# RMSNorm with SiLU: another division of the work over the engines, and loads and stores on two queues

## The chip, the cores and the metric

The kernel runs on one core of a Trainium2 chip. The time is the device time in microseconds of one execution; lower is better. The engines' names in the profile are PE (TensorE), DVE (VectorE), ACT (ScalarE), POOL (GpSimd) and SP (SyncE). They run side by side, each works through its own instructions in their order, and they wait for each other by semaphores. Transfers between HBM and the on-chip memory are done by 16 DMA engines; SP and ACT only issue them.

## The reference

The input x has 8 x 1024 rows of 2048 float32 values. Each row is divided by its root mean square, multiplied by gamma, and passed through SiLU:

```python
rms = np.sqrt(np.mean(x ** 2, axis=-1, keepdims=True) + eps)
out = gamma * x / rms
return (out * (1 / (1 + np.exp(-out)))).astype(np.float32)
```

67.1 MB are read and 67.1 MB written.

## The kernel before

The 8192 rows are cut into 16 blocks (`nblk`) of 512 rows. A block is one tile `xt` of 128 partitions with J = 4 rows each, 4.19 MB, so every partition holds 32 KB that lie together in HBM. The tile is loaded, changed in place and stored. There are 6 such buffers (`BUFS`), and `LEAD` = 5 blocks are loaded ahead.

The work on a block has two parts. `stats(b)` makes the reciprocal root mean square: ACT squares rows 0 to 2 and sums them (L63), DVE does row 3 with a fused multiply and reduce (L59); both write their squares to PSUM tiles that nobody reads. POOL then turns the four sums into the variance (L66) and raises it to the power -0.5 (L69). `finish(b)` multiplies each row by rstd and gamma in one instruction on DVE (L74), and after each second row ACT applies Silu to a pair of rows at once, 4096 values per partition (L78). Then SP issues the store (L79).

The order is written out by hand, under `manual_schedule`: each engine runs its instructions in the order of the program text. The main loop calls `stats(b + 1)` before `finish(b)`, so ACT and DVE sum up the squares of the next block before they finish this one, and rstd of a block is made one step ahead of its use. After `finish(b)` comes `load(b + 5)`.

All loads and stores of x are issued by SP on one queue, in program order. `load(b + 5)` waits until the buffer that it takes is free, which is when store b - 1 has landed; the store of the next block stands behind that wait. Gamma is loaded by ACT's queue into one row of the first buffer and spread over the 128 partitions by POOL (L89).

Of the kernel before, what the change touches and what calls it, by code (L numbers as in the profile page):

```python
# [1 line left out]

# [4 lines left out]

ACT = mybir.ActivationFunctionType
ALU = mybir.AluOpType


@with_exitstack
def kernel(
    ctx: ExitStack,
    tc: tile.TileContext,
    x: bass.AP,
    gamma: bass.AP,
    eps: bass.AP,
    out: bass.AP,
):  # L20

    nc = tc.nc
    P = nc.NUM_PARTITIONS
    f32 = mybir.dt.float32
    x2 = x.flatten_outer_dims()
    o2 = out.flatten_outer_dims()
    n, d = x2.shape
    J = 4  # L30
    BUFS, LEAD = 6, 5
    nblk = n // (P * J)
    xb = x2.rearrange("(b p j) d -> b p (j d)", p=P, j=J)
    ob = o2.rearrange("(b p j) d -> b p (j d)", p=P, j=J)

    singles = ctx.enter_context(tc.tile_pool(name="singles", bufs=1))
    pool = ctx.enter_context(tc.tile_pool(name="pool", bufs=BUFS))
    small = ctx.enter_context(tc.tile_pool(name="small", bufs=4))
    psum = ctx.enter_context(tc.tile_pool(name="psum", bufs=1, space=bass.MemoryType.PSUM))

    g = singles.tile([P, d], f32)
    half = singles.tile([P, J], f32)
    junk_a = psum.tile([P, d], f32, name="junk_a")
    junk_v = psum.tile([P, d], f32, name="junk_v")
    blocks, rstds = {}, {}

    def load(b):
        xt = pool.tile([P, J * d], f32, name="xt")
        nc.sync.dma_start(out=xt, in_=xb[b])  # L49
        blocks[b] = xt  # L50

    def row(b, j):
        return blocks[b][:, j * d:(j + 1) * d]

    def stats(b):
        ss = small.tile([P, J], f32, name="ss")
        for j in range(J):
            if j == J - 1:
                nc.vector.tensor_tensor_reduce(  # L59
                    out=junk_v, in0=row(b, j), in1=row(b, j), scale=1.0, scalar=0.0,  # L60
                    op0=ALU.mult, op1=ALU.add, accum_out=ss[:, j:j + 1])
            else:
                nc.scalar.activation(out=junk_a, in_=row(b, j), func=ACT.Square,  # L63
                                     accum_out=ss[:, j:j + 1])
        var = small.tile([P, J], f32, name="var")
        nc.gpsimd.tensor_scalar(out=var, in0=ss, scalar1=1.0 / d, scalar2=float(eps),  # L66
                                op0=ALU.mult, op1=ALU.add)
        rstd = small.tile([P, J], f32, name="rstd")
        nc.gpsimd.tensor_tensor(out=rstd, in0=var, in1=half, op=ALU.pow)  # L69
        rstds[b] = rstd  # L70

    def finish(b):
        for j in range(J):
            nc.vector.scalar_tensor_tensor(out=row(b, j), in0=row(b, j), scalar=rstds[b][:, j:j + 1],  # L74
                                           in1=g, op0=ALU.mult, op1=ALU.mult)
            if j % 2:
                pair = blocks[b][:, (j - 1) * d:(j + 1) * d]
                nc.scalar.activation(out=pair, in_=pair, func=ACT.Silu)  # L78
        nc.sync.dma_start(out=ob[b], in_=blocks.pop(b))  # L79
        del rstds[b]  # L80

    with tc.manual_schedule():
        grow = pool.tile([P, J * d], f32, name="xt")
        nc.scalar.dma_start(out=grow[0:1, 0:d],
                            in_=bass.AP(tensor=gamma.tensor, offset=gamma.offset, ap=[[d, 1], gamma.ap[0]]))
        for b in range(LEAD):
            load(b)
        nc.gpsimd.memset(half, -0.5)  # L88
        nc.gpsimd.partition_broadcast(g, grow[0:1, 0:d])  # L89
        stats(0)  # L90
        for b in range(nblk):
            if b + 1 < nblk:
                stats(b + 1)
            finish(b)
            if b + LEAD < nblk:
                load(b + LEAD)


# [1 line left out]
_INS = ['x', 'gamma', 'eps']  # L100
_OUTS = [((8, 1024, 2048), 'float32')]

_NUMBERS = {'eps': 9.999999747378752e-06}


# [26 lines left out]
```

## Time and profile before

| | us |
|---|---|
| median of 8 runs | 320.78 (320.63 to 321.87) |
| the profiled execution, its own time | 320.71 |
| span of the profiled execution | 318.9 |
| busy: DVE, ACT, POOL | 181.9, 213.1, 60.2 |
| a 4.19 MB transfer, issue to landing, median: load, store | 29.4, 38.4 |
| first load lands, first store is issued, last store is issued | 13.6, 40.2, 293.5 |

The span is the time from the first to the last thing that the profile records; the reported time is 1.8 us longer. A row of the profile's groups gives line, engine, operation, output and inputs with their shapes, how many there were, their busy time and mean duration in ns, and then how long the engine stood idle before them and what ended most of that. The chain of waits follows the work that ended last backwards: at each step to what released it. A queue's line gives its packets, megabytes and its share of the time of the 16 DMA engines.

### The profile page before, as it was taken

The numbers are of one execution on the slowest core, as the hardware profiler recorded it, in microseconds if no ns is written. First come the engines' busy times: TensorE is split into PE (matmuls) and PEld (weight loads), VectorE is DVE, ScalarE is ACT, GpSimd is POOL, SyncE is SP. The second block draws the span as 40 slices with busy tenths as digits, with TensorE's granted clock in tenths as the row PEclk, the third lists the DMA queues.
The fourth block names the chain that finished last, engine by engine and source line by source line (L and its number), as shares of the span: only waits on it lengthen the run. The fifth ranks groups of instructions, "written<-read, shape, count | busy, mean of one in ns | idle before, by whom it ended". The sixth has DMA issues, their size and how long they took to land.

```text
span 318.9 us, 433 instructions
## 1 busy us (share of the span) xinstructions
DVE 181.9 (57%) x96; ACT 213.1 (67%) x130; POOL 60.2 (19%) x38
## 2 busy tenths in 40 slices
DVE  0208998898629185391854909458093672993000
ACT  1249899999988478384784748757487674876000
POOL 0206324502104004040030402204021040400000
DMA  8999999999999999999999999999999999999993
GB/s 322 423 423 452 403 460 353 436 444 419 448 419 424 452 411 452 407 449 432 423 452 411 440 427 436 440 419 444 423 432 444 415 452 419 440 440 415 456 415 164
DMA packets 4612, 134.24 MB, mean 421 GB/s; under 512 B 513, under 2 KB 513, under 8 KB 513
## 3 DMA queue, kind: packets, MB, share of 16 engines
q1 hardware_dynamic: 4608, 134.22, 98.3%
q14 instruction: 2, 0.02, 0.0%
q10 hardware_dynamic: 2, 0.01, 0.0%
HBM read 67.12 MB, written 67.11 MB: 421 GB/s over the span
## 4 chain that ended last, share of the span: by engine, by line
DMA 74%; DVE 8%; ACT 5%; issue 3%; DVEq 1%; SPq 1%; POOL 0%; ACTq 0%; POOLq 0%
DMA out_dram<-xt 58%; DMA xt<-in_x_dram 16%; DVE xt L74 8%; ACT xt L78 3%; ACT junk_a L63 3%; DVEq L127 1%; SPq L49 1%; POOL rstd L69 0%; DVE ss L59 0%; DVE junk_v L59 0%; DVEq L74 0%; ACTq L63 0%; DVEq L59 0%; SPq L79 0%; POOLq L66 0%
## 5 line engine op out<-in xcount | busy, mean ns | idle before, releaser
L74 DVE SCALAR_TENSOR_TENSOR xt<-xt,rstd,g 128x2048 f32<-128x2048 f32 x64 | 146.1, 2346 | 3.4 <-POOL rstd L69 3.4
L78 ACT ACTIVATE xt<-xt 128x4096 f32<-128x4096 f32 x32 | 115.2, 3613 | 20.8 <-DVE xt L74 20.8
L63 ACT ACTIVATE junk_a<-xt 128x2048 f32<-128x2048 f32 x48 | 90.2, 1880 | 58.2 <-DMA xt<-in_x_dram 57.2
L59 DVE CUSTOM_DVE_ANT_0 junk_v<-xt 128x2048 f32<-128x2048 f32 x16 | 36.8, 2299 | 104.6 <-DMA xt<-in_x_dram 104.6
L66 POOL TENSOR_SCALAR var<-ss 128x4 f32<-128x4 f32 x16 | 19.6, 1226 | 207.1 <-ACT junk_a L63 185.0
L69 POOL TENSOR_TENSOR rstd<-var,half 128x4 f32<-128x4 f32 x16 | 38.0, 2376 | 1.3
L63 ACT ACTIVATION_READ_ACCUMULATOR junk_a<-xt 128x1 f32 x48 | 8.9, 186 | 0.0
L89 POOL PARTITION_BROADCAST g<-xt x1 | 2.3, 2302 | 10.2 <-issue 10.2
L59 DVE DVE_READ_ACCUMULATOR2_ANT ss<- 128x1 f32 x16 | 2.3, 141 | 0.0
L63 ACT ACT_TABLE_LOAD x1 | 1.3, 1283 | 1.3 <-PEq L113 1.3
L78 ACT ACT_TABLE_LOAD x1 | 1.3, 1283 | 0.0
L88 POOL MEMSET half<- 128x4 f32 x1 | 0.1, 102 | 0.3 <-POOLq L113 0.3
L113 POOL MEMSET const-float32-0.0<- 128x1 f32 x1 | 0.1, 99 | 0.2 <-issue 0.2
L113 POOL MEMSET const-bfloat16-1.0<- 128x1 bf16 x1 | 0.1, 103 | 0.0
L113 POOL MEMSET const-uint8-127<- 128x1 uint8 x1 | 0.1, 102 | 0.0
L113 POOL MEMSET const-float32-1.0<- 128x1 f32 x1 | 0.1, 99 | 0.0
## 6 DMA issues: line engine op xcount, KB each, us to landing
xt<-in_x_dram SPq DMA_DIRECT2D x16, 4096.0 KB, 29.4
out_dram<-xt SPq DMA_DIRECT2D x16, 4096.0 KB, 38.4
xt<-in_gamma_dram ACTq DMA_DIRECT2D x1, 8.0 KB
```

Source lines behind the costliest of these rows:

```text
L49: nc.sync.dma_start(out=xt, in_=xb[b])
L59: nc.vector.tensor_tensor_reduce(out=junk_v, in0=row(b, j), in1=row(b, j), scale=1.0, scalar=0.0, op0=ALU.mult, op1=ALU.add, accum_out=ss[ ...
L63: nc.scalar.activation(out=junk_a, in_=row(b, j), func=ACT.Square, accum_out=ss[:, j:j + 1])
L66: nc.gpsimd.tensor_scalar(out=var, in0=ss, scalar1=1.0 / d, scalar2=float(eps), op0=ALU.mult, op1=ALU.add)
L69: nc.gpsimd.tensor_tensor(out=rstd, in0=var, in1=half, op=ALU.pow)
L74: nc.vector.scalar_tensor_tensor(out=row(b, j), in0=row(b, j), scalar=rstds[b][:, j:j + 1], in1=g, op0=ALU.mult, op1=ALU.mult)
L78: nc.scalar.activation(out=pair, in_=pair, func=ACT.Silu)
L88: nc.gpsimd.memset(half, -0.5)
L89: nc.gpsimd.partition_broadcast(g, grow[0:1, 0:d])
L113: nc = _bacc.Bacc("TRN2", target_bir_lowering=False, num_devices=1)
L127: with _tile.TileContext(nc) as tc:
```

## The change

- The third square of a block moves from ACT to DVE: ACT sums rows 0 and 1, DVE rows 2 and 3.
- rstd is made on DVE: variance, a first guess from the bits of the number (a shift and a subtraction), and four Newton steps of three instructions each, 15 instructions on 128 x 4 values.
- DVE multiplies a row by gamma alone; rstd is the scale operand of Silu on ACT, so that Silu runs row by row, four per block instead of two.
- There is no look-ahead any more: one function `work(b)` does squares, rstd, multiplications, Silu and store of one block, and the loop calls it block after block.
- Stores are issued by ACT, after a block's last Silu. SP issues only loads. `LEAD` is 6: load b + 6 takes the buffer of block b and waits for its store. The sixth load is issued at the start behind gamma's use, since gamma's row lies in that buffer.
- Gamma is spread over the partitions by TensorE: four matmuls of a row of ones with 512 values of gamma into PSUM, then copied by DVE. POOL does nothing after the start.

```diff
-    BUFS, LEAD = 6, 5
+    BUFS, LEAD = 6, 6
...
-    def stats(b):
+    def rsqrt(ss):
+        var = small.tile([P, J], f32, name="var")
+        nc.vector.tensor_scalar(out=var, in0=ss, scalar1=1.0 / d, scalar2=float(eps),
+                                op0=ALU.mult, op1=ALU.add)
+        y = small.tile([P, J], f32, name="y")
+        t = small.tile([P, J], f32, name="t")
+        nc.vector.tensor_single_scalar(out=t.bitcast(i32), in_=var.bitcast(i32), scalar=1,
+                                       op=ALU.logical_shift_right)
+        nc.vector.tensor_scalar(out=y.bitcast(i32), in0=t.bitcast(i32), scalar1=-1, scalar2=0x5F375A00,
+                                op0=ALU.mult, op1=ALU.add)
+        for _ in range(4):
+            nc.vector.scalar_tensor_tensor(out=t, in0=y, scalar=-0.5, in1=y, op0=ALU.mult, op1=ALU.mult)
+            nc.vector.tensor_mul(out=t, in0=t, in1=var)
+            nc.vector.scalar_tensor_tensor(out=y, in0=t, scalar=1.5, in1=y, op0=ALU.add, op1=ALU.mult)
+        return y
+
+    def work(b):
         ss = small.tile([P, J], f32, name="ss")
-        for j in range(J):
-            if j == J - 1:
+        for j in (0, 2, 1, 3):
+            if j < J // 2:
+                nc.scalar.activation(out=junk_a, in_=row(b, j), func=ACT.Square,
+                                     accum_out=ss[:, j:j + 1])
+            else:
                 nc.vector.tensor_tensor_reduce(
                     out=junk_v, in0=row(b, j), in1=row(b, j), scale=1.0, scalar=0.0,
                     op0=ALU.mult, op1=ALU.add, accum_out=ss[:, j:j + 1])
...
+        rstd = rsqrt(ss)
         for j in range(J):
-            nc.vector.scalar_tensor_tensor(out=row(b, j), in0=row(b, j), scalar=rstds[b][:, j:j + 1],
-                                           in1=g, op0=ALU.mult, op1=ALU.mult)
-            if j % 2:
-                pair = blocks[b][:, (j - 1) * d:(j + 1) * d]
-                nc.scalar.activation(out=pair, in_=pair, func=ACT.Silu)
-        nc.sync.dma_start(out=ob[b], in_=blocks.pop(b))
-        del rstds[b]
+            nc.vector.tensor_mul(out=row(b, j), in0=row(b, j), in1=g)
+            nc.scalar.activation(out=row(b, j), in_=row(b, j), func=ACT.Silu, scale=rstd[:, j:j + 1])
+        nc.scalar.dma_start(out=ob[b], in_=blocks.pop(b))
...
-        for b in range(LEAD):
+        for b in range(min(LEAD, BUFS - 1)):
             load(b)
-        nc.gpsimd.memset(half, -0.5)
-        nc.gpsimd.partition_broadcast(g, grow[0:1, 0:d])
-        stats(0)
+        nc.vector.memset(ones, 1.0)
+        for c in range(0, d, 512):
+            nc.tensor.matmul(junk_v[:, c:c + 512], ones, grow[0:1, c:c + 512], start=True, stop=True)
+        nc.vector.tensor_copy(out=g, in_=junk_v)
+        load(BUFS - 1)
         for b in range(nblk):
-            if b + 1 < nblk:
-                stats(b + 1)
-            finish(b)
+            work(b)
             if b + LEAD < nblk:
                 load(b + LEAD)
```

More of the change, by code (lines that the diff above doesn't have):

```diff
@@ L25 @@
     P = nc.NUM_PARTITIONS
-    f32 = mybir.dt.float32
+    f32, i32 = mybir.dt.float32, mybir.dt.int32
     x2 = x.flatten_outer_dims()
@@ L37 @@
     pool = ctx.enter_context(tc.tile_pool(name="pool", bufs=BUFS))
-    small = ctx.enter_context(tc.tile_pool(name="small", bufs=4))
+    small = ctx.enter_context(tc.tile_pool(name="small", bufs=2))
     psum = ctx.enter_context(tc.tile_pool(name="psum", bufs=1, space=bass.MemoryType.PSUM))
     g = singles.tile([P, d], f32)
-    half = singles.tile([P, J], f32)
+    ones = singles.tile([1, P], f32)
     junk_a = psum.tile([P, d], f32, name="junk_a")
     junk_v = psum.tile([P, d], f32, name="junk_v")
-    blocks, rstds = {}, {}
+    blocks = {}
     def load(b):
@@ L61, in stats @@
                     op0=ALU.mult, op1=ALU.add, accum_out=ss[:, j:j + 1])
[L62 to L72, printed above, removed]
-        for j in range(J):
-            nc.vector.scalar_tensor_tensor(out=row(b, j), in0=row(b, j), scalar=rstds[b][:, j:j + 1],
-                                           in1=g, op0=ALU.mult, op1=ALU.mult)
-            if j % 2:
-                pair = blocks[b][:, (j - 1) * d:(j + 1) * d]
-                nc.scalar.activation(out=pair, in_=pair, func=ACT.Silu)
-        nc.sync.dma_start(out=ob[b], in_=blocks.pop(b))
-        del rstds[b]
+        rstd = rsqrt(ss)
+        for j in range(J):
+            nc.vector.tensor_mul(out=row(b, j), in0=row(b, j), in1=g)
+            nc.scalar.activation(out=row(b, j), in_=row(b, j), func=ACT.Silu, scale=rstd[:, j:j + 1])
+        nc.scalar.dma_start(out=ob[b], in_=blocks.pop(b))
     with tc.manual_schedule():
```

## The prediction

> **What bounds the kernel now.** I read the page's head and DMA lines first, since 134 MB pass through one core.
>
> ```profile
> span 318.9 us, 433 instructions
> DVE 181.9 (57%) x96; ACT 213.1 (67%) x130; POOL 60.2 (19%) x38
> DMA packets 4612, 134.24 MB, mean 421 GB/s; under 512 B 513, under 2 KB 513, under 8 KB 513
> q1 hardware_dynamic: 4608, 134.22, 98.3%
> ```
>
> One queue keeps the 16 DMA engines busy for 98.3% of the span, while no compute engine passes 67%. So transfers set the time. The view by windows (columns: stretch, its length, busy time and count of each engine, PE clock, DMA share, GB/s) says whether that holds throughout:
>
> ```profile
> 13.60:23.80 10.20, 2.36 (x2) 6.01 (x6) 0.00 (x0) 1.00 0.99 421
> 34.00:53.00 19.00, 17.89 (x11) 18.03 (x10) 5.97 (x3) 1.00 1.00 404
> 83.40:122.60 39.20, 22.70 (x13) 30.67 (x19) 8.32 (x6) 1.00 1.01 437
> 122.60:162.00 39.40, 22.53 (x13) 26.32 (x17) 7.31 (x5) 1.00 0.99 428
> 300.00:319.00 19.00, 0.00 (x0) 0.00 (x0) 0.00 (x0) 1.00 0.74 321
> ```
>
> It does, at 404 to 437 GB/s. The chain of waits confirms it and gives the pace:
>
> ```profile
> 83.81 38.78 DMA out_dram<-xt
> 122.58 0.02 issue
> 122.60 0.33 SPq L49
> 122.93 0.05 issue
> 122.98 39.16 DMA out_dram<-xt
> ```
>
> One link, 39.2 us, is four transfers of 4.19 MB (two loads, two stores): 9.80 us each, 19.6 us for a block. A changed kernel escapes slowing only if it computes a block in less than that, and ends early enough to leave time for the last store. What a block costs is read from the groups by line and one block's timeline:
>
> ```profile
> L74 DVE SCALAR_TENSOR_TENSOR xt<-xt,rstd,g 128x2048 f32<-128x2048 f32 x64 | 146.1, 2346 | 3.4 <-POOL rstd L69 3.4
> L78 ACT ACTIVATE xt<-xt 128x4096 f32<-128x4096 f32 x32 | 115.2, 3613 | 20.8 <-DVE xt L74 20.8
> L63 ACT ACTIVATE junk_a<-xt 128x2048 f32<-128x2048 f32 x48 | 90.2, 1880 | 58.2 <-DMA xt<-in_x_dram 57.2
> L59 DVE CUSTOM_DVE_ANT_0 junk_v<-xt 128x2048 f32<-128x2048 f32 x16 | 36.8, 2299 | 104.6 <-DMA xt<-in_x_dram 104.6
> L63 ACT ACTIVATION_READ_ACCUMULATOR junk_a<-xt 128x1 f32 x48 | 8.9, 186 | 0.0
> L59 DVE DVE_READ_ACCUMULATOR2_ANT ss<- 128x1 f32 x16 | 2.3, 141 | 0.0
> ```
>
> ```profile
> 133.04 1.88 ACT L63 ACTIVATE junk_a<-xt 128x2048 f32<-128x2048 f32 x1 [5.02 <-DMA xt<-in_x_dram]
> 135.07 1.88 ACT L63 ACTIVATE junk_a<-xt 128x2048 f32<-128x2048 f32 x1
> 135.29 9.13 DVE L74 SCALAR_TENSOR_TENSOR xt<-xt,rstd,g 128x2048 f32<-128x2048 f32 x4
> 136.89 0.19 ACT L63 ACTIVATION_READ_ACCUMULATOR junk_a<-xt 128x1 f32 x1
> ```
>
> Squares step by 2.03 us, four L74 rows take 9.13 us. At 135.29 DVE multiplies the block before, whose rstd is long there, while ACT still squares the new one. That overlap is the look-ahead which the change gives up.
>
> **The change, part by part.** *Totals.* DVE gains 16 reductions (16 x 2.44 = 39 us) and 240 tiny steps (about 38 us): some 259 us. ACT loses 16 squares (33 us) and has 64 Silu rows for 32 pairs (+8): some 188 us. POOL loses its 58 us of L66 and L69, which covered nothing. By totals nobody reaches 319 us, so the price can only come from order.
>
> *The order.* ACT runs, in program order: squares of rows 0 and 1, four Silu, the store's issue, then the next block's squares. The store waits for the last Silu, and the next squares stand behind it on ACT. The Newton steps on DVE wait for those squares, the four multiplications stand behind Newton on DVE, and each Silu waits for one of them. This is a closed round, from one store's issue to the next:
> - Store issue: SP's stores take 0.40 us (median), 0.33 to 0.42; gamma's on ACT took 0.51. With handoffs of 0.04 us on both sides (a multiplication ends at 36.54, the Silu starts at 36.58) I take 0.50; ends 0.41 and 0.60.
> - Two squares: 2.03 + 1.88 + 0.19 less the overlap of 0.06: 4.04.
> - Handoff to DVE 0.05.
> - Newton: var, two integer steps and 4 x 3 steps are 15 dependent 128x4 instructions, each waiting for DVE's own count. DVE has no such row before. Near rows: a 128x4 memset on POOL 102 ns, DVE's accumulator read 141, ACT's 186, POOL's fastest 128x4 tensor_scalar 194 (its median, 752, is POOL's own). An accumulator read's end and the next square lie 0.03 apart, the price of a wait. I take 0.16 + 0.03 (between the two accumulator reads): 15 x 0.193 = 2.90. Ends 15 x 0.132 = 1.98 and 15 x 0.224 = 3.36; POOL's median would make 11.7, kept for a rival.
> - Four multiplications: without a scalar operand, near L59's 2.30 rather than L74's 2.346: 9.13 - 4 x 0.046 = 8.95; I take 9.00; ends 8.95 and 9.14.
> - Handoff 0.04, and the last Silu, 2048 wide: half a pair is 1.81, a square 1.88. The scale read per partition is a new operand; L74, which has one, is 46 ns above L59, so 1.93. Ends 1.81 and 2.07.
> Sum 0.50 + 4.04 + 0.05 + 2.90 + 9.00 + 0.04 + 1.93 = **18.46 us**; ends 17.28 and 19.30.
> DVE's two reductions (2 x 2.39 = 4.78 us) start when its fourth multiplication ends, 6.5 us before the squares are through (0.04 + 1.93 + 0.50 + 4.04), so they cost nothing; that cover goes if ACT is over 1.7 us faster.
>
> The Trainium skill ("ScalarE: Activation LUTs", What ACT_TABLE_LOAD costs) states that each per-partition pointer operand adds about 93 ns to an ACTIVATE. By it the Silu would be 1.97 us, the round 18.50 and the end 0.7 us later than below; no row of this trace has such an operand on ACT.
>
> *The start.* Block 0 lands when it did, 13.63 us. Both engines start there, so DVE's reductions end last: 13.63 + 4.78 + 0.05 + 2.90 + 9.00 + 0.04 + 1.93 = 32.3 us for the first store's issue, 8 us before the old one (40.2). Gamma's data packet lies at 1.5 to 2 us and its completion at 2 to 2.5 us in the DMA view, so four matmuls have until 13.63 - 2.3 (the copy of g, at L59's length) = 11.3 us. No PE row bounds them; I cost them at zero behind a cover of 8.8 us, beyond which each microsecond adds one. The Silu table load (1.28 us) lies in ACT's wait for Newton.
>
> *The transfers.* Loads and stores now sit on two queues over the same 16 engines, and with both filled I give each half: a block per 19.6 us either way. Loads 0 to 2 land by 33 us, then load n at about 33 + 19.6 (n - 2): load 15 at 288 us. The compute round reaches block 15 at 32.3 + 14 x 18.46 + 0.5 = 291.2, so no load is waited for, by a margin of 3 us. Load b+6 waits for store b on SP with nothing but loads behind it. In the built order the semaphores also make some stores wait on ACT for older transfers (store 4 for store 1, store 11 for load 12): load 12 lands at 229, store 11 is ready at 235, so this costs nothing unless transfers come 6 us later.
>
> *The end.* Store 15 is issued at 32.3 + 15 x 18.46 = 309.2 us. The 31 transfers before it have landed by 13.6 + 30 x 9.80 = 307.6 if the engines never idle, so it runs alone. The shortest issue to landing of one transfer before was 12.9 us, and the old span ran 1.3 us past its last landing (SP's wait ends at 317.6): 309.2 + 12.9 + 1.3 = 323.4 us. So the span is 28.0 + 16 x round, with the transfers' 318.9 as its floor; they meet at a round of 18.18 us. Before, the profiled execution reported 320.71 for a span of 318.9, 1.8 more, and lies 0.07 below the median 320.78. Prediction 323.4 + 1.8 = **325.2 us**, 1.4% slower.
>
> The Trainium skill speaks against a gain by the second queue: "DMA: Bandwidth & Descriptors", Issuing engines are not separate DMA queues, says that DMAs from several engines interleave on the same 16 engines and only issue time is saved. By it the floor stays 318.9; a run at the best window's rate throughout would say otherwise.
>
> **The rivals.**
> 1. *Transfers stay the bound, not slower.* If the round is under 18.18 us (a tiny DVE step of 0.174 us with its wait, against my 0.193), the last store queues behind others as before and the time is 318.9 + 1.8 = 320.7. For it: the accumulator read of 141 ns gives 0.171 a step. Against: all other terms must then hold to 0.3 us.
> 2. *The round is longer.* At the upper ends, 19.30 us, the span is 28.0 + 308.8 = 336.8, the time 338.6. A Newton step of POOL's median would give a round of 27.3 and 467 us; against it, that is another engine's row, and DVE's shortest is 141 ns.
> 3. *Two queues change the rate.* At 437 GB/s instead of the mean 428 of a link, 32 x 9.80 = 313.6 us become 307.1: floor 312.4, time 314.2, and this needs a round under 17.78 too. At 404 GB/s they become 332.2: span 337.5, time 339.3. Against both: the windows average 430 with loads and stores in turn, and 421 with loads alone.
> 4. *g is late*, if the matmuls take over 8.8 us: at 12 us, 328.4.
>
> **How the numbers follow.** Under 0.2% (0.64 us) this kernel's time can't be told from no change. Chances: forecast (round 18.2 to 19.0, 321.4 to 334) 0.62, rival 1 0.18, rival 2 0.08, rival 3 down 0.06 and up 0.04, rival 4 0.02. The range reaches from 1 us below rival 1's time, 319.7, to a round of about 19.1, 335.5; outside lie rival 3's gain, the far ends and a part of rival 2: 0.06 + 0.10. The likeliest case's own range is 321.4 to 334. Faster by over 0.2%: rival 3's gain and a little of rival 1, 0.10. Within: most of rival 1, 0.15. Slower: the rest, 0.75.
>
> **What will show it.** Rounds of about 18.5 us between store issues on ACT from about 32 us on; tiny DVE steps of 0.16 us; the four multiplications in 9.0; a last store issued near 309 us; DMA share near 1 until about 300 us and then falling before the last store. Wrong, if stores come every 19.6 us with waits for loads (rival 1), if the tiny steps are off by 30 ns (15 x 16 x 0.03 = 7 us), or if the DMA rate with both queues leaves 428 GB/s by over 1%.

## The result and the profile after

The changed kernel takes 319.60 us (median of 11 runs, 319.41 to 319.74) beside 320.75 us for the kernel before on the same chips. The ratio is 0.9962, with a 95% interval of 0.9954 to 0.9971: 0.4% faster, and just below 319.7, the lower end of the range that was given. The profiled execution took 319.63 us, with a span of 317.9 us (before: 320.71 and 318.9).

The head and the queues' lines of the page after the change:

```profile
span 317.9 us, 637 instructions
PE 7.2 (2%) x8; PEld 2.5 (1%) x8; DVE 256.8 (81%) x370; ACT 194.8 (61%) x130; POOL 0.2 (0%) x4
...
q1 hardware_dynamic: 2304, 67.11, 49.4%
q10 hardware_dynamic: 2306, 67.12, 48.9%
```

DVE is busy for 256.8 us, where the totals of the prediction said 259, and ACT for 194.8, where they said 188. Loads (q1) and stores (q10) share the engines evenly. The groups by line, in the page's columns, give the sizes that had no row before:

```profile
L88 ACT ACTIVATE xt<-xt,y 128x2048 f32<-128x2048 f32 x64 | 128.1, 2002 | 92.5 <-DVE xt L87 92.3
L87 DVE TENSOR_TENSOR xt<-xt,g 128x2048 f32<-128x2048 f32 x64 | 142.2, 2284 | 0.0
L61 DVE TENSOR_SCALAR var<-ss 128x4 f32<-128x4 f32 x16 | 2.7, 170 | 28.0 <-ACT junk_a L79 27.9
L72 DVE SCALAR_TENSOR_TENSOR y<-t,y 128x4 f32<-128x4 f32 x64 | 10.4, 162 | 2.2
```

The chain of waits (start, length, what) shows the round from the second store to the third, apart from the tiny DVE steps between the squares and the multiplications:

```profile
50.21 0.34 ACTq L89
50.59 2.01 ACT junk_a L79 x2
52.63 2.01 ACT junk_a L79 x2
54.66 0.18 DVE var L61
...
57.60 8.82 DVE xt L87 x4
66.44 2.01 ACT xt L88
68.47 0.34 ACTq L89
```

The round is 68.47 - 50.21 = 18.26 us, and it keeps this pace from 31.91 us to the last store's issue: 31.91 + 15 x 18.266 = 305.90. The chain holds no wait for a transfer after the first load's landing. The chain before was DMA for 74%; this one is DVE for 58% and ACT for 27%. The end is seen in the windows (length, busy time and count of PE, PEld, DVE, ACT, POOL, PE clock, DMA share, GB/s) and in the timeline's last row:

```profile
300.00:304.00 4.00, 0.00 (x0) 0.00 (x0) 3.83 (x2) 3.60 (x3) 0.00 (x0) 1.00 0.93 401
304.00:306.00 2.00, 0.00 (x0) 0.00 (x0) 0.00 (x0) 1.87 (x1) 0.00 (x0) 1.00 0.04 16
306.00:308.00 2.00, 0.00 (x0) 0.00 (x0) 0.00 (x0) 0.00 (x0) 0.00 (x0) 1.00 0.88 377
314.00:316.00 2.00, 0.00 (x0) 0.00 (x0) 0.00 (x0) 0.00 (x0) 0.00 (x0) 1.00 1.22 524
316.00:318.00 2.00, 0.00 (x0) 0.00 (x0) 0.00 (x0) 0.00 (x0) 0.00 (x0) 1.00 0.00 0
```

```profile
305.90 0.34 ACTq L89 DMA_DIRECT2D out_dram<-xt  x1
```

The DMA engines have done 31 transfers by 304, stand idle for 2 us, then run the last store alone, 4.19 MB in the 10 us from 306 to 316, and move nothing after that. So the forecast mechanism is there, and yet the kernel is faster. The kernel before ends in another way (windows, with DVE, ACT and POOL as the engines):

```profile
312.00:314.00 2.00, 0.00 (x0) 0.00 (x0) 0.00 (x0) 1.00 0.72 311
314.00:316.00 2.00, 0.00 (x0) 0.00 (x0) 0.00 (x0) 1.00 0.23 98
316.00:318.00 2.00, 0.00 (x0) 0.00 (x0) 0.00 (x0) 1.00 0.08 33
```

Its engines never stand idle, but they don't finish together: for about 5 us only a part of them still moves data. Two questions follow. Does the closed round really set the end now? And what lowered the floor of 318.9 us, below which the prediction let nothing fall?

### The profile page after: what moved, and what is told of

It reads as the page before. It is cut to its first block, busy times and chain, and to the rows that moved or that the text cites. A ratio compares the mean times of both kernels' runs of the same rounds, so it can differ in the third digit from the quotient of the medians.

```text
span 317.9 us, 637 instructions
## 1 busy us (share of the span) xinstructions
PE 7.2 (2%) x8; PEld 2.5 (1%) x8; DVE 256.8 (81%) x370; ACT 194.8 (61%) x130; POOL 0.2 (0%) x4
## 4 chain that ended last, share of the span: by engine, by line
DVE 58%; ACT 27%; issue 4%; DMA 4%; ACTq 2%; DVEq 1%
DVE xt L87 44%; ACT junk_a L79 17%; ACT xt L88 10%; DMA xt<-in_x_dram 4%; DVE t L70 3%; DVE t L71 3%; DVE y L72 3%; ACTq L89 2%; DVE junk_v L82 1%; DVE var L61 1%; DVE y L67 1%; DVE t L65 1%; DVEq L136 1%; DVE ss L82 0%; DVEq L61 0%
## 5 line engine op out<-in xcount | busy, mean ns | idle before, releaser
L88 ACT ACTIVATE xt<-xt,y 128x2048 f32<-128x2048 f32 x64 | 128.1, 2002 | 92.5 <-DVE xt L87 92.3
L87 DVE TENSOR_TENSOR xt<-xt,g 128x2048 f32<-128x2048 f32 x64 | 142.2, 2284 | 0.0
L82 DVE CUSTOM_DVE_ANT_0 junk_v<-xt 128x2048 f32<-128x2048 f32 x32 | 73.5, 2296 | 1.8 <-DMA xt<-in_x_dram 1.3
L79 ACT ACTIVATE junk_a<-xt 128x2048 f32<-128x2048 f32 x32 | 60.2, 1881 | 17.3 <-DMA xt<-in_x_dram 10.5
L61 DVE TENSOR_SCALAR var<-ss 128x4 f32<-128x4 f32 x16 | 2.7, 170 | 28.0 <-ACT junk_a L79 27.9
L70 DVE SCALAR_TENSOR_TENSOR t<-y 128x4 f32<-128x4 f32 x64 | 10.4, 162 | 2.2
L72 DVE SCALAR_TENSOR_TENSOR y<-t,y 128x4 f32<-128x4 f32 x64 | 10.4, 162 | 2.2
L71 DVE TENSOR_TENSOR t<-t,var 128x4 f32<-128x4 f32 x64 | 10.3, 162 | 2.2
L99 PE MATMUL junk_v<-xt,ones 1*128 1x512 f32 x8 | 7.2, 1072 | 2.5 <-DMA xt<-in_gamma_dram 2.5
L79 ACT ACTIVATION_READ_ACCUMULATOR junk_a<-xt 128x1 f32 x32 | 6.0, 186 | 0.0
```

The source lines that it names most:

```text
L61: nc.vector.tensor_scalar(out=var, in0=ss, scalar1=1.0 / d, scalar2=float(eps), op0=ALU.mult, op1=ALU.add)
L70: nc.vector.scalar_tensor_tensor(out=t, in0=y, scalar=-0.5, in1=y, op0=ALU.mult, op1=ALU.mult)
L71: nc.vector.tensor_mul(out=t, in0=t, in1=var)
L72: nc.vector.scalar_tensor_tensor(out=y, in0=t, scalar=1.5, in1=y, op0=ALU.add, op1=ALU.mult)
L82: nc.vector.tensor_tensor_reduce(out=junk_v, in0=row(b, j), in1=row(b, j), scale=1.0, scalar=0.0, op0=ALU.mult, op1=ALU.add, accum_out=ss[ ...
L87: nc.vector.tensor_mul(out=row(b, j), in0=row(b, j), in1=g)
```

## The experiments

All medians in us; each ratio is to the kernel before, run beside it.

| run | time | ratio, 95% interval | span of the profiled run |
|---|---|---|---|
| changed kernel | 319.60 | 0.9962 (0.9954 to 0.9971) | 317.9 |
| newton6 | 338.64, one run | | 336.9 |
| newton2 | 319.84 (318.1 to 323.6) | 0.995 (0.9928 to 0.9973) | 318.5 |
| before_store_act | 321.22 (319.4 to 332.7) | 0.9976 (0.996 to 0.9991) | 317.8 |
| after_one_queue | 321.72 | 1.0027 (1.0014 to 1.0039) | 319.0 |
| after_lead5 | 319.52 | 0.9976 (0.9966 to 0.9985) | 317.8 |
| copy_one | 320.68 | 0.9986 (0.9972 to 1.0) | 318.5 |
| copy_two | 316.87 | 0.9868 (0.9839 to 0.9896) | 315.2 |
| split_last | 319.39 | 0.9947 (0.9926 to 0.9967) | 317.5 |
| split_halves | 319.00 | 0.9956 (0.9944 to 0.9969) | 317.3 |
| newton2_split_last | 321.05 (319.7 to 323.7) | 0.9996 (0.9971 to 1.0021) | 320.4 |
| after_lookahead | 319.41 | 0.9967 (0.9954 to 0.998) | 317.1 |
| silu_plain | 318.82, one run | | 317.0 |

### Is the closed round the limit? newton6 and newton2

```diff
-        for _ in range(4):
+        for _ in range(6):      # newton6;  range(2) in newton2
```

> The changed kernel with six Newton iterations, six tiny DVE steps more per block: round 18.27 + 1.18 = 19.45 us. Theory A: the first store 1.2 us and the last 16 x 1.18 = 18.9 us later, span 336.8, time 338.5. Theory B (transfers set the end; the round has slack up to the transfers' 19.6 us a block): under 322.

> The changed kernel with two Newton iterations in place of four, so six tiny DVE steps of 0.196 us less per block: round 18.27 - 1.18 = 17.09 us. Theory A (the compute round sets the end: last store's issue at 305.9, 12.0 us more to the end): the last store could be issued at 31.9 - 1.2 + 15 x 17.09 = 287, so the round stops binding and the transfers' own end shows, 31 transfers through at 304.3 as now, 9.8 for the last and 2 to the end: span 316, time 317.8, about 1.8 us below the changed kernel's 319.6. Theory B (transfers set the end already, the compute round is only level with them): 319.6, unchanged. In between if the engines end raggedly again, as before the change.

Measured: newton6 took 338.64 us where Theory A said 338.5 and Theory B under 322. Its page's head and the last row of its timeline:

```profile
span 336.9 us, 735 instructions
```

```profile
324.91 0.34 ACTq L89 DMA_DIRECT2D out_dram<-xt  x1
```

The last store was issued 19.0 us later than in the changed kernel and again 12.0 us before the end of the span. So a longer round costs 16 times its growth (16 x 1.18 = 18.9): upwards the forecast's rule holds, in the one run that was made of it.

Downwards it does not. newton2 should have issued its last store at 287 us; it did so at 304.87, 1.0 us earlier than the changed kernel. Its timeline and its list of waits (engine, line, for what: us in total, times, longest) say what came in the way:

```profile
267.96 1.88 ACT L79 ACTIVATE junk_a<-xt 128x2048 f32<-128x2048 f32 x1 [2.19 <-DMA xt<-in_x_dram]
...
287.38 1.88 ACT L79 ACTIVATE junk_a<-xt 128x2048 f32<-128x2048 f32 x1 [1.97 <-DMA xt<-in_x_dram]
```

```profile
DVE junk_v L82 <- DMA xt<-in_x_dram: 31.4, 9, 4.8
```

Nine blocks now wait for their loads, where in the changed kernel only the first does. The last two of these loads arrive 19.4 us apart, the last at 287.4. One block of compute behind it takes 17.5 us (DVE's two reductions, which nothing covers here, then Newton, the multiplications and the last Silu) and gives 304.9. Both theories hold in part: the round sets the end of the changed kernel, but the arrival of loads lies only just behind it. The changed kernel's block 15 starts at 288.03, right behind the store of block 14. In time the two can't be told apart: the interval of newton2's ratio overlaps that of the change.

### What lowered the floor? copy_one and copy_two

```diff
     def work(b):
-        ss = small.tile([P, J], f32, name="ss")
...
-        nc.scalar.dma_start(out=ob[b], in_=blocks.pop(b))
+        nc.sync.dma_start(out=ob[b], in_=blocks.pop(b))      # copy_one, with LEAD = 5; copy_two keeps nc.scalar
```

> The same copy without computation, loads and stores on SP's queue, five blocks ahead. The floor of the transfers with one queue: 320.7 if the kernel before was bound by transfers alone and its ragged end comes with the queue; less by as much as its late stores cost it otherwise.

> No computation on x at all (squares, rstd, multiplications and Silu left out; output is x): loads on SP's queue, stores on ACT's queue, each store as soon as its load has landed. The floor of the transfers with two queues. If two queues move data faster by themselves: 316 to 318. If not: 320.7, as the one-queue copy beside it.

Measured: 320.68 and 316.87 us. The one-queue copy takes as long as the whole kernel before (ratio 0.9986): the kernel before was bound by its transfers alone. The two-queue copy is 3.8 us, 1.2%, faster for the same bytes, on the same 16 engines. The windows of copy_one (length, PE, PEld, DVE, POOL, clock, DMA share, GB/s):

```profile
40.00:290.00 250.00, 0.00 (x0) 0.00 (x0) 0.00 (x0) 0.00 (x0) 1.00 1.00 430
312.00:314.00 2.00, 0.00 (x0) 0.00 (x0) 0.00 (x0) 0.00 (x0) 1.00 0.84 360
314.00:316.00 2.00, 0.00 (x0) 0.00 (x0) 0.00 (x0) 0.00 (x0) 1.00 0.27 115
316.00:318.00 2.00, 0.00 (x0) 0.00 (x0) 0.00 (x0) 0.00 (x0) 1.00 0.04 16
```

and of copy_two:

```profile
40.00:290.00 250.00, 0.00 (x0) 0.00 (x0) 0.00 (x0) 0.00 (x0) 1.00 1.00 432
312.00:314.00 2.00, 0.00 (x0) 0.00 (x0) 0.00 (x0) 0.00 (x0) 1.00 0.38 164
314.00:316.00 2.00, 0.00 (x0) 0.00 (x0) 0.00 (x0) 0.00 (x0) 1.00 0.00 0
```

In the middle the rates differ by 432 to 430 GB/s, which over 250 us is worth 250 x 2 / 430 = 1.2 us. The end is worth more. At 312 us copy_one has 2 x (360 + 115 + 16) = 982 KB left, which at its rate is 2.3 us of work, and its span ends 6.5 us later, at 318.5. copy_two has 2 x 164 = 328 KB left, 0.8 us of work, and ends 3.2 us later, at 315.2. So of the 3.3 us between the two spans 1.8 are a shorter ragged end, and 1.5 are the 654 KB that copy_two is ahead at 312. The time to issue a transfer has no part in this end, since copy_one issues its last store 49 us before it:

```profile
269.25 0.33 SPq L76 DMA_DIRECT2D out_dram<-xt  x1
```

Three limits of this reading. The rate isn't shown to be the queue's: in the same 250 us the other profiles, one of each version, show 430 to 433 GB/s on two queues (newton6, which leaves the engines idle at times, 428) and 430 to 431 on one. The end differs in the same way in most of the kernels that compute, but not in all: taken as above, what the end costs beyond its work is 4.8 us in the kernel before and 5.6 in after_one_queue, and on two queues about 4 in before_store_act, split_last, split_halves and newton2, but 5.8 in newton2_split_last. And the copies differ in more than the queue: loads run five blocks ahead in one and six in the other, and on one queue a store stands behind the wait of the load before it. Why the engines end closer together, no run shows.

### Is it the queue, in the real kernels? after_one_queue, after_lead5, before_store_act

```diff
-    BUFS, LEAD = 6, 6
+    BUFS, LEAD = 6, 5
...
-        nc.scalar.dma_start(out=ob[b], in_=blocks.pop(b))
+        nc.sync.dma_start(out=ob[b], in_=blocks.pop(b))      # after_one_queue; left out in after_lead5
...
-        load(BUFS - 1)
```

> The changed kernel with its stores back on SP and loads five blocks ahead, as before the change: one queue for all. If the second queue makes the gain: 320.7 or more, with the old ragged end. If the round alone sets the end: the last store is issued at 305.9 again and ends 12.0 us later, 319.6.

> The changed kernel with loads five blocks ahead instead of six, still on two queues. The one-queue version of the changed kernel (321.7) had this distance too. If the queue made its difference: 319.6 here, or a little more if a load comes late. If the shorter distance made it: 321.7.

Measured: 321.72 us (ratio 1.0027) with one queue, 319.52 us (ratio 0.9976) with two, at the same distance of loads. These two kernels differ in one line, the engine that issues the stores, and the intervals of their ratios, each to the kernel before on its own chip, lie apart: that line makes the difference, 0.5%. The distance makes none that the intervals show (0.9976 beside the change's 0.9962). The one-queue version issued its last store 8 us earlier than the changed kernel and still ended later, so here an early last store was worth nothing:

```profile
297.97 0.33 SPq L89 DMA_DIRECT2D out_dram<-xt  x1
```

The same line alone was changed in the kernel before:

```diff
-        nc.sync.dma_start(out=ob[b], in_=blocks.pop(b))
+        nc.scalar.dma_start(out=ob[b], in_=blocks.pop(b))    # in the kernel before: before_store_act
```

> The kernel before with one line changed: stores are issued by ACT, loads stay on SP. Look-ahead, POOL's rstd and paired Silu stay. If the second queue by itself makes the gain (other order of transfers, engines that end together): 319.6 or less, 0.9962 of before. If queues don't matter and the gain came from the earlier stores and the new compute order: 320.7, ratio 1.000.

Measured: the profiled run has a span of 317.8 us. Its eleven times lie in two groups, six from 319.4 to 321.2 and five from 328.9 to 332.7, and the ratio of 0.9976 is that of the first. So this one line brings a gain of about the size of the whole change's in some executions and a loss of 3% in others. What makes the second group stays open; no profile of it was taken.

### Where the gap to 316.9 lies: split_last, split_halves, newton2_split_last

```diff
+            if b == nblk - 1:
+                nc.sync.dma_start(out=ob[b][:, j * d:(j + 1) * d], in_=row(b, j))
+        if b < nblk - 1:
-        nc.scalar.dma_start(out=ob[b], in_=blocks.pop(b))
+            nc.scalar.dma_start(out=ob[b], in_=blocks.pop(b))
```

split_halves does the same after rows 1 and 3, with two rows at a time; newton2_split_last is split_last with two iterations.

> The changed kernel, but the last block is stored row by row, four stores of 1 MB, each issued by SP as soon as its Silu is through. In the changed kernel the engines stand nearly idle from 304 to 306 us and then run 12.0 us for the last store alone. Theory A (the compute round and the lone last store set the end): the last row's store is issued at 306 still, but only a quarter of 9.8 us is left to move by then; rows 0 to 2 (from 299.3 us on) fill the gap; limit becomes the transfers, 304.3 + 9.8 + about 2: span 316, time 317.8. If the transfers themselves set the end: no change, 319.6.

> The changed kernel with the last block stored in two halves by SP (rows 0 and 1 at 301.6 us, rows 2 and 3 at 305.9). Alone, the second half needs 4.9 + 2.2 us after 305.9: 313, so the transfers decide: 316 to 317.5 span, 317.8 to 319.4. By rows it was 319.4; if fewer, larger stores end more evenly: under that. If the lone last store isn't what sets the end: 319.6.

> Both: two Newton iterations and the last block stored by rows. Two iterations alone gave times from 318.1 to 323.6, its last block waiting for its load. If a late last load followed by one block of compute is what spreads those times, rows stored early take back some 7 us of each: 316 to 318, with little spread. If the transfers spread by themselves: 318 to 323 again.

Measured: 319.39, 319.00 and 321.05 us. The idle 2 us are gone in both split versions; from split_last's windows:

```profile
304.00:306.00 2.00, 0.00 (x0) 0.00 (x0) 0.00 (x0) 1.82 (x1) 0.00 (x0) 1.00 0.99 418
312.00:314.00 2.00, 0.00 (x0) 0.00 (x0) 0.00 (x0) 0.00 (x0) 0.00 (x0) 1.00 0.77 324
314.00:316.00 2.00, 0.00 (x0) 0.00 (x0) 0.00 (x0) 0.00 (x0) 0.00 (x0) 1.00 0.06 25
```

But the span falls by 0.4 to 0.6 us only, not by the 1.9 expected: an end without a pause is again a ragged one. In the changed kernel the lone last store, which all engines start after the same pause, doesn't show this. split_halves has the lowest median of the versions that compute everything, but its interval overlaps that of the change, so it isn't shown to be better. With two iterations the early stores of rows did not take the spread away, against the expectation: 319.7 to 323.7. What spreads the transfers there is open.

### The look-ahead, and Silu's operand: after_lookahead and silu_plain

```diff
         for b in range(nblk):
+            if b + 1 < nblk:
+                sums(b + 1)         # squares and sums of work(b + 1)
             work(b)
```

> The changed kernel with the look-ahead put back: squares of block b+1 are issued on ACT and DVE before block b's rstd and multiplications. The round is open then: DVE needs 2 x 2.39 + 2.9 + 8.9 = 16.6 us a block. Theory A (the closed round of 18.27 us sets the end, above a floor of 316.9 that the two-queue copy shows): 316.9 to 318.5. Rival (without the round as a brake the stores crowd the loads and the last block waits for its load, as with two Newton iterations): 318 to 323, with a spread of several us.

Measured: 319.41 us, ratio 0.9967, which can't be told from the change's 0.9962. With the look-ahead back, DVE waits for loads ten times (once in the changed kernel), and the last store is issued at 305.13 instead of 305.90:

```profile
DVE junk_v L82 <- DMA xt<-in_x_dram: 29.7, 10, 4.9
```

The rival had the limit right (the last block waits for its load) and the spread wrong (318.87 to 319.52). The closed round thus costs next to nothing here: without it the last store comes only 0.8 us earlier, since the arrival of loads then holds the kernel.

```diff
-            nc.scalar.activation(out=row(b, j), in_=row(b, j), func=ACT.Silu, scale=rstd[:, j:j + 1])
+            nc.scalar.activation(out=row(b, j), in_=row(b, j), func=ACT.Silu)
```

> The changed kernel with Silu's scale operand left out (an immediate 1 in its place), so rstd is computed but not applied. If the operand read per partition is what makes a Silu 2002 ns beside the square's 1881: Silu 1881, round 18.27 - 0.12 = 18.15, last store issued 16 x 0.12 = 1.9 us earlier, at 304.0; the span then 316.0 if the round sets the end alone, 316 to 318 if the transfers take over. If Silu itself is slower than Square: 2002 as before and the same span, 317.9.

```profile
L88 ACT ACTIVATE xt<-xt 128x2048 f32<-128x2048 f32 x64 | 122.2, 1910 | 96.9 <-DVE xt L87 96.9
```

Measured: 1910 ns, so the operand costs 2002 - 1910 = 92 ns. The other 29 ns above Square are not shown to be the function's, since Square writes to PSUM and Silu doesn't. The last store came at 304.45, 1.45 us earlier (16 x 0.092 = 1.47), but the span fell by 0.9 only: the pause before the last store shrank, and the transfers before it began to count.

## Why the prediction was wrong

Two steps failed: sizes in the sum, and the floor under it.

The sum, 28.0 + 16 x round, gave a span of 323.4 us, 5.5 more than the 317.9 measured. Three of its terms were too large: the round, 18.46 for 18.27, 15 times (2.9 us); the end after the last store's issue, 12.9 + 1.3 for 12.0 (2.2); the first store's issue, 32.3 for 31.9 (0.4). Its shape was right: stores come one round apart, no load is waited for, and the last store runs alone. That the measured terms, 31.9 + 15 x 18.27 + 12.0, make 317.9 is no evidence for it, since they are parts of that span; newton6 is, where the shape with the measured terms said 338.5 and 338.64 came.

The floor was put as "So the span is 28.0 + 16 x round, with the transfers' 318.9 as its floor". It took the old kernel's end for a property of the bytes, and it belonged to the single queue: the two-queue copy ends its span at 315.2, and the changed kernel with its stores back on SP's queue at 319.0. With every term of the sum right, this floor would still have raised 317.9 to 318.9, a time of 320.7, and said "no change". The only gain that was considered, in rival 3, named the right part with another mechanism: it asked for 437 GB/s throughout and got a chance of 0.06 at most. What came is a mid-run rate of 433 GB/s, where the kernel before has 431 (40 to 290 us, one profile of each), and an end without the ragged tail.

Point by point:

- *Transfers bound the kernel before.* Right: its copy without computation takes 320.68 us.
- *The round, 18.46 us.* Right in kind, 0.2 too long: 18.26. Store issue with handoffs 0.41 (0.50 said), squares 4.05 (4.04), handoff 0.02 (0.05), Newton 2.86 (2.90), multiplications 8.89 (9.00), handoff 0.04, Silu 2.00 (1.93). A tiny step takes 162 to 170 ns and comes every 0.196 us (0.193 said). Silu, 0.07 too short, hides a part of the rest.
- *The end, 12.9 + 1.3 after the last issue.* Mis-sized: 12.0, in the changed kernel and in newton6 alike. The 12.9 was that of the first load, at the start.
- *31 transfers landed by 307.6.* Too late: they are through by about 304. The sum counted one block by 13.6 us, and by then 5.0 MB had moved (367 GB/s over 13.6 us), with other loads part done. The last store ran alone either way.
- *DVE's reductions are covered by 1.7 us.* Right: L61 waits 27.9 us in 15 blocks for the squares, 1.9 each.
- *g is ready in time.* Right: the matmuls end at 9.6 us, the copy at 12.0.
- *No load is waited for, by 3 us.* Right for this kernel, but the margin was thin: newton2, with a round 1.2 us shorter, waited for nine, the first among them.
- *The Trainium skill on the pointer operand* ("ScalarE: Activation LUTs", What ACT_TABLE_LOAD costs): about 93 ns stated, 92 measured (2002 against 1910 ns); its Silu of 1.97 us was nearer to the 2.00 measured than mine of 1.93.
- *The Trainium skill on the second queue* ("DMA: Bandwidth & Descriptors", Issuing engines are not separate DMA queues): it says that only the sequencer's issue time is saved. The two copies differ by 3.8 us, at a DMA share of 1.00 in both from 40 to 290 us, and the one-queue copy has issued everything by 269.6 us; after_one_queue and after_lead5 differ by 2.2. So issue time can't be the cause, and the measurement decides against the rule here.

So the gain is the second queue's: the floor falls by 3.3 us of span, from copy_one's 318.5 to copy_two's 315.2. The changed kernel ends 2.7 us above the new floor. Its closed round sets where it ends, but that 2.7 is not shown to be the price of the round: the old order on two queues has a span of 317.8 (before_store_act, its profiled run), the look-ahead put back 317.1, and no profiled run of a version that computes came nearer to the floor than silu_plain's 317.0.

## What to carry to other kernels

A span full of transfers at a DMA share of 1.00 need not be at its floor: look at the last 10 us of the windows, where a rate that falls off in steps shows engines that don't end together, and measure the floor by a copy without computation, once for each arrangement of queues. A compute round that closes on itself costs its growth times the number of blocks once its last store is issued after all other transfers are through (here from the round of 18.27 us up to newton6's 19.44, still under the transfers' 19.6 a block). A shorter round brings little: the compute of one block behind the last load takes its place. Where a term has no row, a nearer row than "the shortest of its kind" is worth the search: the first load's 12.9 us was no price for a store at the end.

## What the runs showed of the hardware that was not expected

- The same 134 MB copy takes 320.68 us on one queue and 316.87 us on two.
- A store of 4.19 MB that starts on idle engines ends the span 12.0 us after its issue, twice (305.90 to 317.9, 324.91 to 336.9); no ragged end is seen behind it.
- Times of one kernel with stores on a second queue can spread widely: 318.1 to 323.6 (newton2), 319.7 to 323.7 (newton2_split_last), 319.4 to 332.7 (before_store_act). Others stay together: 319.41 to 319.74 (the changed kernel), 318.87 to 319.52 (after_lookahead), 316.63 to 317.44 (copy_two). The last two have no closed round, so the round is not shown to be what holds the times together; the cause of the spread is open.
